# Linear attention on quarters of the TensorE array, with small matmuls kept together in the schedule

## The chip, the cores and the metric

One core of a Trainium2 chip. The metric is the device time of one execution in microseconds (us); the inputs and weights lie in the chip's main memory (HBM), the activations stay on chip. The kernel was run three times before the change: 1510.91, 1511.21 and 1512.28 us, median 1511.21. A further execution was taken with the profiler, and all rows of this document ahead of the result come from that one.

## The reference

A trunk of two layers over 512 tokens of width 1024, all in f32. Each layer: RMS norm, a mixer, a residual sum, an MLP of width 4096 with squared ReLU, then an embedding term gated by a sigmoid. Layer 1's mixer is block attention. Layer 0's mixer has two halves, 512 channels each: a gated scan ("hgrn", 4 heads of 128, computed in chunks) and the linear attention with a delta rule that the change touches ("rwkv", 8 heads of 64 channels):

```
def step(state, inp):
    r_t, w_t, k_t, v_t, kk_t, a_t = inp
    sa = einsum('bhvk,bhk->bhv', state, -kk_t)
    state = (state * w_t[:, :, None, :]
             + sa[..., None] * (kk_t * a_t)[:, :, None, :]
             + v_t[..., None] * k_t[:, :, None, :])
    return state, einsum('bhvk,bhk->bhv', state, r_t)
```

So every token's state row is decayed by w, corrected by a rank one term (kk, a) and written by (v, k), and read by r. Afterwards each head is normalised, a bonus term is added, and both halves go through one output projection.

## The kernel before

Activations lie with channels on the 128 partitions and the 512 tokens in the free dimension. All large products go through `gemm` (L248), which calls `mm3` (L243 to L246): weights and activations are split in a high and a low part of type fp32r, and each product is three matmuls of 128x128 weights by 512 streamed columns. `wnext` (L222) loads the weights on SyncE's queue (SP), and ScalarE (ACT, L236) and VectorE (DVE, L237) split them. Small jobs (the linear attention, the gated scan, statistics, transposes) use plain f32 or f16 matmuls on TensorE (PE), with their results in three rings of PSUM banks: `pj` (2 banks, gemm), `pmh` (2, gated scan) and `pmr` (4, linear attention). GpSimd (POOL) clears buffers and does some elementwise work.

The linear attention works on 4 pairs of heads (`hp`), 128 channels each, so each head has half of the partitions (`hs[h]`). The 512 tokens of a pair are taken in two halves (`g`) of 4 chunks of 64 tokens; two chunks side by side make a block `a`. There are so 8 units (hp, g). The steps of a unit:

- `pre` (L526), once for a pair: decays, the normalised key kk, beta's rows `bh`, k's rows `kh`, the receptance `rh_` and the query-like `al` (both in `ar`).
- `p1` (L588): the scores. Beta's rows of both heads are copied by ACT into `BH` (L596), whose other blocks are zero, so that one matmul for each chunk with all 128 partitions (L600) gives both heads' scores; the same for k's rows. DVE masks them into `NA` and `KA` (L605), again beside zero blocks. Four transposes for each block (L614) give `TOK` and, through ACT (L619), `BZ`, also with zero blocks. L625 and L631 multiply k's scores with v; ACT writes the second into y (L632).
- `p2` (L635): a triangular solve in f16 with five doublings (L664 to L670), one refinement in f32 (L676 to L685), and the product with the tokens (L690), copied into `MU` (L693).
- `p3` (L698): the maps of each chunk's state, on the whole array with `BZ` (L707 to L711), masked into `GB` by DVE (L714) and scaled into `HS` by ACT (L718); `inner` (L723), two groups of four matmuls with 64 columns of weights (L726, L731), added by DVE into rh_ and y (L727, L732); `states` (L735), one matmul and two DVE operations for each chunk; then the state's share of y (L754).
- `tail` (L759): normalisation and gate, and the split for the output projection.

The order of the work comes from a scheduler that builds each engine's list of instructions ahead of time, by priority among what is ready by its own cost figures. A priority follows the order of the program; `run` (L786) puts its generators 300 places ahead (`OFS`), and `weave` (L347) interleaves two generators. `ORDER` = "AFHBOC" (L33) sets the steps for each pair: A is p2 of the first half beside p3 and tail of the pair before and p1 of the second half; F and H are the projections and the gated scan; B the projections of the next pair; O the output projection of the pair before; C p2 of the second half beside `pre` of the next pair and p3 of the first half, then p1 of the next pair. Gemm passes are ranked behind and fill what PE has free. `Stats.add` (L289, L291) and `bcast_rows` (L326, L334) are helpers with groups of four small matmuls, used in both layers.

Of the kernel before, what the change touches and what calls it, by code (L numbers as in the profile page):

```python
# [12 lines left out]
F32 = mybir.dt.float32  # L13
# [6 lines left out]
OP = mybir.AluOpType  # L20
# [14 lines left out]
OFS = 300  # L35
NWARM = 9

P = 128
# [147 lines left out]
def trunk(ctx, tc, wts, xT, pT, vecs, lora, cst, lev, seg, rope, gain, out, upto="all", dbg=None, mode=None):  # L186
# [97 lines left out]
    class Stats:  # L284
# [4 lines left out]
        def add(self, sq, rhs):  # L289
            for j in range(NJ):  # L290
                T.matmul(self.ps[:, j * self.cols:(j + 1) * self.cols], sq[:, j * P:(j + 1) * P], rhs,  # L291
                         start=(self.i == 0 and j == 0), stop=(self.i == self.n - 1),
                         skip_group_check=True)
            self.i += 1
# [31 lines left out]
    def bcast_rows(rt, cols, pool, tag):  # L326
        ps = pool.tile([P, S], F32, name=tag)
        if cols > 1:
            full = nrm.tile([P, S], F32, name="bc")
            V.tensor_copy(full.rearrange("p (c w) -> p c w", w=P // cols),  # L330
                          rt[:, :, None].to_broadcast([P, NJ * cols, P // cols]))
        for j in range(NJ):
            lhs = full[:, j * P:(j + 1) * P] if cols > 1 else rt[:, j:j + 1].to_broadcast([P, P])
            T.transpose(ps[:, j * P:(j + 1) * P], lhs, ident)  # L334
        return ps
# [28 lines left out]
    def layer0_mixer(actp):  # L364
        ph = ExitStack()
        mp = ph.enter_context(tc.tile_pool(name="mp", bufs=1))
        BH = mp.tile([P, 2, 4, P], F32, name="BH")
        NAs = [mp.tile([P, 2, 2, 2, P], F32, name=f"NA{i}") for i in range(2)]
        KAs = mp.tile([P, 2, 2, 2, P], F32, name="KA")
        BZ = [mp.tile([P, 2, 2, 2, P], F32, name=f"BZ{i}") for i in range(2)]  # L370
# [3 lines left out]
        early = [BH, KAs, *NAs, *BZ, GB, SB, PP]  # L374
# [141 lines left out]
        def four(lhs, rhs):  # L516
            ps = pmr.tile([P, S], F32, name="pmr")
            for i in range(4):
                T.matmul(ps[:, i * P:i * P + P], lhs(i), rhs(i), start=True, stop=True)
            return ps.rearrange("p (i t) -> p i t", i=4)  # L520
# [5 lines left out]
        def pre(hp, r, k, v):  # L526
# [38 lines left out]
            V.tensor_mul(kk, kk, ps)  # L565
            yield
# [9 lines left out]
            V.tensor_mul(bh, bh, pi)  # L576
# [5 lines left out]
            V.tensor_mul(kh, kh, pi)  # L582
            pre_[hp] = (lw, bh, kh, ar, rh_, bo, dl, v, E("y", 2))
# [4 lines left out]
        def p1(hp, g):  # L588
            lw, bh, kh, ar, rh_, bo, dl, v, y = pre_[hp]
            gs = slice(g * 256, g * 256 + 256)  # L590
            NA, KA, TOK = NAs[g], KAs, []
            un[hp, g] = (NA, TOK)

            for n, (src, dst) in enumerate(((bh, NA), (kh, KA))):
                for h in range(2):
                    A.copy(BH[hs[h], n, :, hs[h]], src[hs[h], gs].rearrange("p (c t) -> p c t", t=64))  # L596
                ps = pmr.tile([P, S], F32, name="pmr")
                for c_ in range(4):
                    o = g * 256 + c_ * 64
                    T.matmul(ps[:, c_ * P:c_ * P + P].rearrange("p (x t) -> p x t", x=2), BH[:, n, c_, :],  # L600
                             ar[:, :, o:o + 64], start=True, stop=True)
                pv = ps.rearrange("p (a c x t) -> p a c x t", a=2, c=2, x=2)
                for h in range(2):
# [3 lines left out]
                yield  # L607
            for a in range(2):
# [4 lines left out]
                for n, src in enumerate((ar[:, 0, :], v, bh, kh)):  # L613
                    T.transpose(ps[:, n * P:n * P + P], src[:, js], ident)  # L614
# [9 lines left out]
            for i, (a, h) in enumerate(pk):  # L624
                T.matmul(ps[:, i * 64:i * 64 + 64], KA[:, a, h, 0, :], TOK[a][:, 1, hs[h]], start=True, stop=True)  # L625
            for a in range(2):
                A.copy(TOK[a][:, 2, :], ps[:, a * P:a * P + P])
            yield
            ps = pmr.tile([P, S], F32, name="pmr")
            for i, (a, h) in enumerate(pk):  # L630
                T.matmul(ps[hs[h], a * P:a * P + P], TOK[a][:, 1, hs[h]], KA[:, a, h, 1, :], start=True, stop=True)  # L631
            A.copy(y[:, gs], ps[:, :256])  # L632
            yield

        def p2(hp, g):  # L635
# [3 lines left out]
            for a in range(2):  # L639
                A.copy(n16[:, 2 * a:2 * a + 2, :], NA[:, a, :, 0, :])  # L640
# [6 lines left out]
            for l in range(1, 6):  # L647
# [12 lines left out]
                def half4(lhs, rhs):  # L660
                    ps = pmr.tile([P, S], F32, name="pmr")
                    pv = ps[:, :256].rearrange("p (i n u) -> p i n u", i=4, u=H)
                    for i in range(4):
                        T.matmul(pv[:, i], lhs[:, i, :], rhs[:, i], start=True, stop=True)  # L664
# [10 lines left out]
            for i, (a, h) in enumerate(pk):  # L675
                T.matmul(ps[:, i * P:i * P + P], NA[:, a, h, 0, :], tt[:, i, :], start=True, stop=False)  # L676
                T.matmul(ps[:, i * P:i * P + P], id16, id16, start=False, stop=True)
# [4 lines left out]
            for i in range(4):  # L682
                T.matmul(ps[:, i * P:i * P + P], er[:, i, :], XT[:, i, :], start=True, stop=False)
                T.matmul(ps[:, i * P:i * P + P], id16, XT[:, i, :], start=False, stop=True)
# [4 lines left out]
            for i, (a, h) in enumerate(pk):  # L689
                T.matmul(ps[:, i * P:i * P + P].rearrange("p (x f) -> p x f", x=2), tt[:, i, :],  # L690
                         TOK[a][:, 0::2, hs[h]], start=True, stop=True)
            MU = E("MU", 2, [P, 2, 2, P])
            A.copy(MU.rearrange("p a x (h f) -> p a h x f", h=2),  # L693
                   ps.rearrange("p (a h x f) -> p a h x f", a=2, h=2, x=2))
            un[hp, g] = (NA, TOK, MU)
            yield

        def p3(hp, g):  # L698
            lw, bh, kh, ar, rh_, bo, dl, v, y = pre_[hp]
            NA, TOK, MU = un.pop((hp, g))  # L700
# [3 lines left out]
            for a in range(2):  # L704
                bz = BZ[g][:, a]
                ps = pmr.tile([P, S], F32, name="pmr")
# [5 lines left out]
                pv = ps.rearrange("p (x c f) -> p x c f", x=2, c=2)  # L712
                for h in range(2):
                    V.tensor_tensor(GB[hs[h], 2 * a:2 * a + 2, hs[h]], pv[hs[h], 0, :, hs[h]],  # L714
                                    cc("istack")[hs[h], None, :].to_broadcast([64, 2, 64]), op=OP.add)
                    for c_ in range(2):
                        ch = 4 * g + 2 * a + c_
                        A.activation(HS[hs[h], 2 * a + c_, :], pv[hs[h], 1, c_, hs[h]], AF.Copy,  # L718
                                     scale=dl[hs[h], ch:ch + 1])
                yield  # L720


            def inner():  # L723
                ps = pmr.tile([P, S], F32, name="pmr")
                for i, (a, h) in enumerate(pk):
                    T.matmul(ps[hs[h], a * P:a * P + P], MU[:, a, 0, hs[h]], NA[:, a, h, 1, :], start=True, stop=True)  # L726
                V.tensor_add(rh_[:, gs], rh_[:, gs], ps[:, :256])  # L727
                yield
                ps = pmr.tile([P, S], F32, name="pmr")
                for i, (a, h) in enumerate(pk):  # L730
                    T.matmul(ps[hs[h], a * P:a * P + P], MU[:, a, 1, hs[h]], NA[:, a, h, 1, :], start=True, stop=True)  # L731
                V.tensor_add(y[:, gs], y[:, gs], ps[:, :256])  # L732
# [19 lines left out]
            for c_ in range(f, 4):  # L752
                ch = 4 * g + c_
                T.matmul(ps[:, c_ * 64:c_ * 64 + 64], SB[:, ch, :], rh_[:, ch * 64:ch * 64 + 64], start=True, stop=True)  # L754
# [4 lines left out]
        def tail(hp):  # L759
            lw, bh, kh, ar, rh_, bo, dl, v, y = pre_.pop(hp)  # L760
# [37 lines left out]
        def hgrn(h, q, ff, iv, gproj):  # L798
# [3 lines left out]
            for j in range(NJ):  # L802
                T.transpose(ps[:, j * P:j * P + P], iv[:, j * P:j * P + P], ident)
# [25 lines left out]
            for j in range(NJ):  # L829
                js = slice(j * P, j * P + P)  # L830
                T.matmul(ps[:, js], ks[:, js], d[:, js], start=True, stop=True)
            V.copy_predicated(at, m8[:, 13, None, :].to_broadcast([P, NJ, P]), j4(ps))
            for l in range(2, 7):
# [15 lines left out]
                for j in range(NJ):  # L849
                    js = slice(j * P, j * P + P)  # L850
# [496 lines left out]
```

## Time and profile before

| | us |
|---|---|
| median of 3 runs | 1511.21 |
| the profiled execution | 1511.89 |
| its span, first to last instruction | 1510.1 |
| PE busy | 1478.1 (98%) |
| DVE busy | 937.6 (62%) |
| ACT busy | 663.1 (44%) |
| POOL busy | 138.4 (9%) |

The span is what the profile covers, and all windows and starts are counted from its beginning. PE's busy time is made of matmul records that overlap, so work is better counted from one start to the next. An f32 matmul has two records, a transpose, an f16 or an fp32r matmul has one. PEld is PE's loading of weights, which overlaps its matmuls. The layer 0 mixer ends near 440 us.

### The profile page before, as it was taken

Reading aid. Unit: us, or ns where it says so; the run is one execution under the profiler, and the core shown is the slowest. Engines: PE = TensorE matmul, PEld = TensorE weight load, DVE = VectorE, ACT = ScalarE, POOL = GpSimd, SP = SyncE. Lnnn points to the kernel's source line nnn. Section 1 sums busy time; section 2 is a strip of 40 time slices with the busy share of each in tenths; the row PEclk is TensorE's granted clock in tenths of the full one; section 3 lists DMA queues with packets and bytes.
Section 4 is the critical chain, followed back from the end, with each engine's and each line's share of the span. In section 5 each row is a group of like instructions: output and inputs, shape, how many; then the busy total and the mean of one; then the engine's idle time right before and its main releaser. Section 6 shows DMA issues by size and latency. Waiting matters only on the chain.

```text
span 1510.1 us, 20495 instructions
## 1 busy us (share of the span) xinstructions
PE 1478.1 (98%) x7546; PEld 1191.3 (79%) x7546; DVE 937.6 (62%) x1835; ACT 663.1 (44%) x1269; POOL 138.4 (9%) x133
## 2 busy tenths in 40 slices
PE   8899999999989999999999999999999999999998
PEld 6678777777667888888888888777778888888887
DVE  6878797687785664444446648377575444445463
ACT  4675545554446433333334534455634333333342
POOL 4121220310205000000000200000220000000000
PEclk9999999999999999999999999999999999999999
DMA  5110111211123233333333432221123333333331
GB/s 179 56 36 22 55 50 39 66 29 47 39 91 106 90 98 98 98 98 98 98 95 98 124 118 84 77 63 50 56 80 95 95 101 98 98 96 93 98 98 70
DMA packets 67109, 123.88 MB, mean 82 GB/s; under 512 B 7632, under 2 KB 8016, under 8 KB 67008
## 3 DMA queue, kind: packets, MB, share of 16 engines
q1 hardware_dynamic: 65376, 118.57, 25.6%
q10 hardware_dynamic: 1152, 2.43, 0.5%
q0 software_dynamic: 480, 1.57, 0.3%
q8 instruction: 59, 0.97, 0.3%
q14 instruction: 42, 0.34, 0.1%
HBM read 120.45 MB, written 2.10 MB: 81 GB/s over the span
## 4 chain that ended last, share of the span: by engine, by line
PE 87%; DVE 7%; ACT 3%; issue 2%; DMA 1%; POOL 1%; SPq 0%; DVEq 0%; ACTq 0%; POOLq 0%
PE pj L244 20%; PE pj L246 20%; PE pj L245 20%; PE pmr L1273 1%; PE pmr L245 1%; PE pmr L1249 1%; PE pmr L246 1%; PE pmr L244 1%; PE pj L1176 1%; PE pmr L1176 1%; PE pj L1178 1%; PE pmr L1177 1%; PE pmr L1178 1%; PE pj L1177 1%; PE pmh L1176 1%
## 5 line engine op out<-in xcount | busy, mean ns | idle before, releaser
L236 ACT CAST whi<-wr 128x512 fp32r<-128x512 f32 x428 | 265.0, 621 | 549.2 <-PE pj L245 421.9
L237 DVE TENSOR_TENSOR wlo<-wr,whi 128x512 fp32r<-128x512 f32 x428 | 312.5, 733 | 197.6 <-ACT whi L236 193.6
L244 PE MATMUL pj<-act,whi 128*128 128x512 f32 (+1 forms) x856 | 338.1, 396 | 1.2 <-DVE h L935 1.0
L245 PE MATMUL pj<-act,whi 128*128 128x512 f32 (+1 forms) x856 | 336.8, 394 | 0.0
L246 PE MATMUL pj<-act,wlo 128*128 128x512 f32 (+1 forms) x856 | 335.7, 393 | 0.5 <-DVE wlo L237 0.5
L244 PE MATMUL pj<-hid,whi 128*128 128x512 f32 x512 | 199.2, 389 | 0.0
L245 PE MATMUL pj<-hid,whi 128*128 128x512 f32 x512 | 199.2, 389 | 0.0
L246 PE MATMUL pj<-hid,wlo 128*128 128x512 f32 x512 | 199.2, 389 | 0.0
L244 PEld LDWEIGHTS pj<-act,whi 128*128 128x128 f32 x856 | 161.1, 188 | 34.4 <-ACT k L491 1.4
L246 PEld LDWEIGHTS pj<-act,wlo 128*128 128x128 f32 x856 | 161.2, 188 | 32.5 <-DVE wlo L237 1.5
L245 PEld LDWEIGHTS pj<-act,whi 128*128 128x128 f32 x856 | 161.2, 188 | 31.1 <-issue 1.5
L1115 DVE TENSOR_TENSOR x<-x,pj 128x512 f32<-128x512 f32 x128 | 88.0, 688 | 80.6 <-PE pj L246 80.2
L245 PEld LDWEIGHTS pj<-hid,whi 128*128 128x128 f32 x512 | 96.1, 188 | 20.0
L244 PEld LDWEIGHTS pj<-hid,whi 128*128 128x128 f32 x512 | 96.1, 188 | 19.9
L246 PEld LDWEIGHTS pj<-hid,wlo 128*128 128x128 f32 x512 | 96.1, 188 | 19.9
L319 POOL TENSOR_TENSOR acc<-acc,xsq 128x512 f32<-128x512 f32 x35 | 48.7, 1393 | 628.8 <-ACT xsq L313 616.0
L1104 DVE SCALAR_TENSOR_TENSOR r<-pj,rb 128x512 f32<-128x512 f32 x56 | 38.7, 691 | 84.0 <-PE pj L246 84.0
L278 DVE TENSOR_TENSOR hid<-r,hid 128x512 fp32r<-128x512 f32 x64 | 44.3, 691 | 41.5 <-ACT hid L277 41.4
L1105 ACT ACTIVATE r<-r 128x512 f32<-128x512 f32 x64 | 40.5, 632 | 21.6 <-DVE r L1104 21.5
L277 ACT CAST hid<-r 128x512 fp32r<-128x512 f32 x64 | 39.8, 621 | 1.9
L280 ACT ACTIVATE act<-x,vec 128x512 fp32r<-128x512 f32 x32 | 22.9, 720 | 29.4 <-DVE x L1133 12.7
L244 PE MATMUL pj<-os,whi 128*128 128x512 f32 x64 | 28.3, 445 | 4.4 <-DVE x L946 2.8
(387 smaller groups left out, 2225.8 us busy)
## 6 DMA issues: line engine op xcount, KB each, us to landing
wr<-in_wts_dram SPq DMA_DIRECT2D x428, 256.0 KB, 2.7
x<-in_xT_dram SPq DMA_DIRECT2D x8, 256.0 KB, 6.3
sr<-in_wts_dram SPq DMA_DIRECT2D x8, 256.0 KB, 5.3
out_dram<-x SPq DMA_DIRECT2D x7, 256.0 KB, 2.0
r<-in_pT_dram ACTq DMA_DIRECT2D x4, 256.0 KB, 3.0
lw<-in_lora_dram POOLq DMA_DIRECT2D x4, 192.0 KB, 3.1
tq<-in_rope_dram ACTq DMA_DIRECT2D x1, 512.0 KB, 6.7
tk<-in_rope_dram ACTq DMA_DIRECT2D x1, 512.0 KB, 7.6
```

Of the source, the lines that this page charges most:

```text
L236: A.copy(hi, raw)
L237: V.tensor_sub(lo, raw, hi.bitcast(F32))
L244: T.matmul(ps, wh, xh, start=first, stop=False)
L245: T.matmul(ps, wh, xl, start=False, stop=False)
L246: T.matmul(ps, wl, xh, start=False, stop=last)
L277: A.copy(h, src)
L278: V.tensor_sub(l, src, h.bitcast(F32))
L319: G.tensor_add(self.t, self.t, sq)
L1104: V.scalar_tensor_tensor(r, q, 0.0, nf[0], op0=OP.max, op1=OP.mult)
L1105: A.activation(r, r, AF.Square)
L1115: V.tensor_add(x[k], x[k], ps)
L1176: T.matmul(ps[j], xh, wh, start=k == 0, stop=False)
```

## The change

Scores are computed on quarters of the array: a matmul takes one head's 64 partitions and writes 64 partitions of the output, 16 of them for a unit instead of 8, into two banks `pq`, one for each head. Which half of the output partitions it writes depends on the chunk (`c_`), and is the other one for k's rows (`c_ ^ n`). Beta's and k's rows lie in one tile `bk`, chunk by chunk, so that one transpose (still two for each block) brings both to the partitions of a chunk (`BKs`). `W` holds for each chunk the solved rows on one half of the partitions and v's rows on the other (v with its chunks swapped is `vx`), so the separate product with v (L631) falls away: `p3` and `inner` contract over both at once, with 64 columns of weights and 64 streamed columns. BH, BZ and MU go; NA and KA lose the part that is now in `RRs`. HS is scaled by one DVE operation, the first write of y in `inner` becomes an ACT copy.

`tight()` ranks instructions 40 places ahead. It is put around the new groups and, besides them, around the small groups of `Stats.add`, `bcast_rows`, `four`, `half4`, the refinement, the state's share of y, and the gated scan (`hgrn`).

The diff, cut to its core:

```diff
+TIGHT = 40
+    def tight():
+        return tc.high_priority(offset=TIGHT)
...
         def add(self, sq, rhs):
-            for j in range(NJ):
-                T.matmul(self.ps[:, j * self.cols:(j + 1) * self.cols], sq[:, j * P:(j + 1) * P], rhs,
+            with tight():
+                for j in range(NJ):
+                    T.matmul(self.ps[:, j * self.cols:(j + 1) * self.cols], sq[:, j * P:(j + 1) * P], rhs,
...
-        BH = mp.tile([P, 2, 4, P], F32, name="BH")
-        NAs = [mp.tile([P, 2, 2, 2, P], F32, name=f"NA{i}") for i in range(2)]
-        KAs = mp.tile([P, 2, 2, 2, P], F32, name="KA")
-        BZ = [mp.tile([P, 2, 2, 2, P], F32, name=f"BZ{i}") for i in range(2)]
+        NAs = [mp.tile([P, 2, 2, P], F32, name=f"NA{i}") for i in range(2)]
+        KAs = mp.tile([P, 2, 2, P], F32, name="KA")
+        RRs = [mp.tile([P, 2, 2, 2, 64], F32, name=f"RR{i}") for i in range(2)]
+        BKs = [mp.tile([P, 2, 2, P], F32, name=f"BK{i}") for i in range(2)]
+        Ws = [mp.tile([P, 2, 2, 2, P], F32, name=f"W{i}") for i in range(2)]
...
+            vx = E("vx", 1)
+            for c_ in range(2):
+                A.copy(vx.rearrange("p (j c t) -> p j c t", c=2, t=64)[:, :, 1 - c_],
+                       v.rearrange("p (j c t) -> p j c t", c=2, t=64)[:, :, c_])
...
-            for n, (src, dst) in enumerate(((bh, NA), (kh, KA))):
-                for h in range(2):
-                    A.copy(BH[hs[h], n, :, hs[h]], src[hs[h], gs].rearrange("p (c t) -> p c t", t=64))
...
-                    T.matmul(ps[:, c_ * P:c_ * P + P].rearrange("p (x t) -> p x t", x=2), BH[:, n, c_, :],
-                             ar[:, :, o:o + 64], start=True, stop=True)
...
+            pq = [pmr.tile([P, S], F32, name="pmr").rearrange("p (c a x t) -> p c a x t", c=2, a=2, x=2)
+                  for h in range(2)]
+            with tight():
+                for a in range(2):
                     for c_ in range(2):
-                        V.tensor_tensor(dst[hs[c_], :, h, :, hs[c_]], pv[hs[h], :, c_, :, :],
-                                        tri[hs[h], None, :, :].to_broadcast([64, 2, 2, 64]), op=OP.mult)
+                        o = g * 256 + a * P + c_ * 64
+                        for n in range(2):
+                            at = bk[:, 2 * g + a, 3 * c_ if n == 0 else 1 + c_, :]
+                            for h in range(2):
+                                T.matmul(pq[h][hs[c_ ^ n], c_, a], at[hs[h]], ar[hs[h], :, o:o + 64],
+                                         start=True, stop=True)
...
-                for c_ in range(2):
-                    A.copy(BZ[g][hs[c_], a, :, c_, :], pv[hs[c_], 2:4, :])
+                A.copy(BKs[g][:, a], pv[:, 2:4, :])
+                for c_ in range(2):
+                    A.copy(W_[hs[1 - c_], a, c_, 1, :], pv[hs[1 - c_], 1, :])
...
-                T.matmul(ps[hs[h], a * P:a * P + P], TOK[a][:, 1, hs[h]], KA[:, a, h, 1, :], start=True, stop=True)
-            A.copy(y[:, gs], ps[:, :256])
...
-                T.matmul(ps[:, :256], MU[:, a, 0, :], bz[:, 0].rearrange("p c f -> p (c f)"), start=True, stop=True)
-                for c_ in range(2):
-                    o = ps[:, 256 + c_ * P:256 + c_ * P + P]
-                    T.matmul(o, bz[:, 0, c_, :], MU[:, a, 1, :], start=True, stop=False)
-                    T.matmul(o, bz[:, 1, c_, :], TOK[a][:, 1, :], start=False, stop=True)
...
+            with tight():
+                for k in range(4):
+                    a, c_ = divmod(k, 2)
+                    for h in range(2):
+                        T.matmul(pv[hs[h], k, 0], W_[:, a, c_, 0, hs[h]], BKs[g][:, a, c_, hs[h]], start=True, stop=True)
+                    for h in range(2):
+                        T.matmul(pv[hs[h], k, 1], BKs[g][:, a, c_, hs[h]], W_[:, a, c_, 1, hs[h]], start=True, stop=True)
...
-                        A.activation(HS[hs[h], 2 * a + c_, :], pv[hs[h], 1, c_, hs[h]], AF.Copy,
-                                     scale=dl[hs[h], ch:ch + 1])
+            V.tensor_tensor(HS, pv[:, :, 1, :], dl[:, 4 * g:4 * g + 4, None].to_broadcast([P, 4, 64]), op=OP.mult)
...
-                    T.matmul(ps[hs[h], a * P:a * P + P], MU[:, a, 0, hs[h]], NA[:, a, h, 1, :], start=True, stop=True)
...
-                    T.matmul(ps[hs[h], a * P:a * P + P], MU[:, a, 1, hs[h]], NA[:, a, h, 1, :], start=True, stop=True)
-                V.tensor_add(y[:, gs], y[:, gs], ps[:, :256])
+                with tight():
+                    for x_ in range(2):
+                        for a in range(2):
+                            for c_ in range(2):
+                                for h in range(2):
+                                    T.matmul(pv[hs[h], x_, 2 * a + c_], W_[:, a, c_, x_, hs[h]], RR[:, a, h, c_, :],
+                                             start=True, stop=True)
+                yield
                 V.tensor_add(rh_[:, gs], rh_[:, gs], ps[:, :256])
+                A.copy(y[:, gs], ps[:, 256:])
```

## Rows read from the trace of the kernel before

**Rows 1.** The page: busy share of PE, and its granted clock in 40 slices.
```profile
PE 1478.1 (98%) x7546; PEld 1191.3 (79%) x7546; DVE 937.6 (62%) x1835; ACT 663.1 (44%) x1269; POOL 138.4 (9%) x133
...
PEclk9999999999999999999999999999999999999999
```

**Rows 2.** Windows; columns: stretch, length, busy us (instructions) of each engine, clock, DMA.
```profile
65.00:345.00 280.00, 272.95 (x1993) 216.99 (x1992) 220.02 (x527) 159.81 (x363) 54.62 (x54) 1.00 0.14 42
345.00:430.00 85.00, 79.20 (x537) 60.06 (x536) 62.05 (x156) 35.47 (x81) 10.54 (x10) 1.00 0.15 44
...
120.00:160.00 40.00, 38.85 (x340) 32.36 (x340) 32.83 (x96) 22.22 (x59) 3.76 (x4) 1.00 0.11 30
200.00:220.00 20.00, 19.37 (x160) 15.36 (x159) 18.04 (x49) 8.41 (x17) 5.60 (x7) 1.00 0.12 35
...
440.00:445.00 5.00, 4.72 (x15) 3.44 (x15) 2.67 (x6) 1.75 (x3) 0.00 (x0) 0.75 0.34 109
```

**Rows 3.** Timeline of PE: start, length, line, out<-in, weights, streamed, records [idle before <-releaser].
```profile
64.26 2.02 PE L600 MATMUL pmr<-ar,BH 128*128 128x128 f32 x16 [0.96 <-issue]
66.12 0.27 PE L614 MATMUL pmr<-cs,ar 128*128 128x128 f32 x1
...
69.05 0.43 PE L631 MATMUL pmr<-KA,TOK 128*64 128x128 f32 x2
69.41 0.49 PE L245 MATMUL pj<-act,whi 128*128 128x512 f32 x1
...
76.77 1.08 PE L625 MATMUL pmr<-TOK,KA 128*128 128x64 f32 x8
77.78 0.66 PE L631 MATMUL pmr<-KA,TOK 128*64 128x128 f32 x8
78.38 0.29 PE L664 MATMUL pmr<-PP,XT 128*128 128x64 f16 x4
...
94.12 0.59 PE L707 MATMUL pmr<-BZ,MU 128*128 128x256 f32 x2
...
95.44 0.83 PE L831 MATMUL pmh<-h 128*128 128x128 f32 x6
...
134.43 0.44 PE L631 MATMUL pmr<-KA,TOK 128*64 128x128 f32 x4
134.80 0.29 PE L664 MATMUL pmr<-PP,XT 128*128 128x64 f16 x4
...
438.14 0.72 PE L244 MATMUL pj<-os,whi 128*128 128x512 f32 x2 [1.65 <-ACT os L277]
```

**Rows 4.** Weight loads of two lines: count, shortest/median/longest ns, first and last start, form.
```profile
L726 PEld LDWEIGHTS pmr<-NA,MU x64: 132/137/138, 110.2 to 414.5; 128*64 128x64 f32 x64
...
L600 PEld LDWEIGHTS pmr<-ar,BH x128: 186/192/193, 64.2 to 345.9; 128*128 128x128 f32 x128
```

**Rows 5.** DVE groups, 35 to 430 us: count | busy us, mean ns | idle before, releaser.
```profile
L605 DVE TENSOR_TENSOR NA<-pmr,cs 64x256 f32<-64x256 f32 x32 | 13.5, 420 | 1.9 <-PE pmr L600 1.5
...
L714 DVE TENSOR_TENSOR GB<-pmr,cs 64x128 f32<-64x128 f32 x32 | 9.2, 288 | 21.5 <-PE pmr L711 18.6 <-ACT HS L718 2.4
...
L732 DVE TENSOR_TENSOR y<-y,pmr 128x256 f32<-128x256 f32 x8 | 3.4, 419 | 3.0 <-PE pmr L731 2.9
```

**Rows 6.** ACT groups of the same stretch.
```profile
L718 ACT ACTIVATE HS<-pmr,dl 64x64 f32<-64x64 f32 x64 | 16.4, 303 | 18.0 <-DVE GB L714 17.1
...
L619 ACT COPY BZ<-pmr 64x256 f32<-64x256 f32 x32 | 11.7, 366 | 0.2
...
L596 ACT COPY BH<-bh 64x256 f32<-64x256 f32 x16 | 6.4, 402 | 8.4 <-PE pmr L600 4.3 <-DVE bh L576 4.0
...
L617 ACT COPY TOK<-pmr 128x256 f32<-128x256 f32 x16 | 5.9, 372 | 2.2 <-PE pmr L614 1.9
...
L693 ACT COPY MU<-pmr 128x512 f32<-128x512 f32 x8 | 4.7, 584 | 6.8 <-PE pmr L690 6.8
...
L627 ACT COPY TOK<-pmr 128x128 f32<-128x128 f32 x16 | 3.4, 267 | 1.2 <-PE pmr L625 1.1
```

More of the change, by code (lines that the diff above doesn't have):

```diff
@@ L517, in four @@
             ps = pmr.tile([P, S], F32, name="pmr")
-            for i in range(4):
-                T.matmul(ps[:, i * P:i * P + P], lhs(i), rhs(i), start=True, stop=True)
+            with tight():
+                for i in range(4):
+                    T.matmul(ps[:, i * P:i * P + P], lhs(i), rhs(i), start=True, stop=True)
             return ps.rearrange("p (i t) -> p i t", i=4)
@@ L638, in p2 @@
             n16 = E("n16", 1, [P, 4, P], F16)
-            for a in range(2):
-                A.copy(n16[:, 2 * a:2 * a + 2, :], NA[:, a, :, 0, :])
+            A.copy(n16, NA.rearrange("p a h t -> p (a h) t"))
             X = E("X", 1, [P, 4, P], F16)
@@ L662, in half4 @@
                     pv = ps[:, :256].rearrange("p (i n u) -> p i n u", i=4, u=H)
-                    for i in range(4):
-                        T.matmul(pv[:, i], lhs[:, i, :], rhs[:, i], start=True, stop=True)
+                    with tight():
+                        for i in range(4):
+                            T.matmul(pv[:, i], lhs[:, i, :], rhs[:, i], start=True, stop=True)
                     return pv
@@ L688, in p2 @@
             ps = pmr.tile([P, S], F32, name="pmr")
[L689 to L695, printed above, removed]
+            with tight():
+                for i, (a, h) in enumerate(pk):
+                    T.matmul(ps[:, i * P:i * P + P].rearrange("p (x f) -> p x f", x=2), tt[:, i, :],
+                             TOK[a][:, 0::2, hs[h]], start=True, stop=True)
@@ L751, in p3 @@
             f = 1 if g == 0 else 0
-            for c_ in range(f, 4):
-                ch = 4 * g + c_
-                T.matmul(ps[:, c_ * 64:c_ * 64 + 64], SB[:, ch, :], rh_[:, ch * 64:ch * 64 + 64], start=True, stop=True)
+            with tight():
+                for c_ in range(f, 4):
+                    ch = 4 * g + c_
+                    T.matmul(ps[:, c_ * 64:c_ * 64 + 64], SB[:, ch, :], rh_[:, ch * 64:ch * 64 + 64], start=True, stop=True)
             yg = y[:, g * 256 + f * 64:g * 256 + 256]
@@ L828, in hgrn @@
             ps = pmh.tile([P, S], F32, name="pmh")
-            for j in range(NJ):
-                js = slice(j * P, j * P + P)
-                T.matmul(ps[:, js], ks[:, js], d[:, js], start=True, stop=True)
+            with tight():
+                for j in range(NJ):
+                    js = slice(j * P, j * P + P)
+                    T.matmul(ps[:, js], ks[:, js], d[:, js], start=True, stop=True)
             V.copy_predicated(at, m8[:, 13, None, :].to_broadcast([P, NJ, P]), j4(ps))
@@ L848, in hgrn @@
                 ps = pmh.tile([P, S], F32, name="pmh")
-                for j in range(NJ):
-                    js = slice(j * P, j * P + P)
-                    T.matmul(ps[:, j * 64:j * 64 + 64], ks[:, js], qs[:, j * 64:j * 64 + 64], start=True, stop=True)
+                with tight():
+                    for j in range(NJ):
+                        js = slice(j * P, j * P + P)
+                        T.matmul(ps[:, j * 64:j * 64 + 64], ks[:, js], qs[:, j * 64:j * 64 + 64], start=True, stop=True)
                 def hi(t):
@@ L871, in hgrn @@
             ps = pmh.tile([P, S], F32, name="pmh")
-            for j in range(3):
-                T.matmul(ps[:, j * P:j * P + P], kt[:, j * P:j * P + P], vt[:, j, :], start=True, stop=True)
+            with tight():
+                for j in range(3):
+                    T.matmul(ps[:, j * P:j * P + P], kt[:, j * P:j * P + P], vt[:, j, :], start=True, stop=True)
             st_ = Hh()
```

130 lines of the change are left out of this document (73 added, 57 removed).

## The prediction

> **What bounds the kernel now.** I read the page's busy shares and slices first, then windows of the stretch that the diff touches, then the timeline of TensorE inside it, then the groups of VectorE and ScalarE there. The page shows TensorE (PE) busy in 98% of the span and at full clock almost throughout [rows 1]. The linear attention and the gated scan beside it lie between 35 and about 440 us. In the windows from 65 to 430 us PE is busy for 352.2 of 365 us, VectorE (DVE) for 282.1, ScalarE (ACT) for 195.3 [rows 2]. So PE bounds this stretch. But DVE is close in places: 32.8 of 40 us where the chains of two head pairs meet (120 to 160 us), 18.0 of 20 us in the window from 200 to 220 us [rows 2]. A microsecond taken from PE is therefore a microsecond of time only while DVE, and the chain PE to DVE to ACT and back, still keep up.
>
> How PE's time is counted: start to start, not by the busy durations, which hold a pipeline's tail. An f32 matmul is two records. Sixteen records of the old scores (128 columns streamed, whole array) take from 64.26 to 66.12 us, 0.116 us each [rows 3]. Eight records with only 64 columns streamed (L625) take from 76.77 to 77.78 us, 0.126 each including the way into the next group [rows 3]: halving the streamed columns alone gains nothing when 128 columns of weights are loaded. The weight loads differ: median 192 ns for 128 columns, 137 ns for 64 [rows 4], so 64 columns of weights cost 55 ns and 128 cost 110, which is what the small matmuls are paced by.
>
> The rows that matter most are those of matmuls that fill half of the array's columns (L631). One such matmul alone (x2) takes from 69.05 to 69.41 us, 0.36; two, one in each half (x4), from 134.43 to 134.80, 0.37; four (x8), from 77.78 to 78.38, 0.60 [rows 3]. The second is free: the halves run side by side. Two further pairs of records cost 0.23 us, so a slot of two records of 128 streamed columns takes about 0.11, and a group of four slots has 0.60 - 0.42 = 0.18 us of edges at 0.105 a slot. The entry from whole-array work costs some 0.09 more: L625's eight records at 0.112 would have ended 0.9 us after their start, and the gap is 1.01 [rows 3]. A group that uses part of the array thus costs 0.27 us plus its slots.
>
> **The change, part by part.** There are eight units, one for each of 4 head pairs and 2 halves of the sequence.
>
> Scores (p1). Removed: 8 matmuls, 16 records, 1.86 us [rows 3]. Added: 16 matmuls of 64 rows by 64 columns, 32 records; four neighbours lie on four different quarters of the array. No row shows quarters split by rows. Bounds: if all four run side by side, 8 slots, 0.84 + 0.27 = 1.11 us; if only column halves do, 16 slots, 1.68 + 0.27 = 1.95; if none do, 32 slots, 3.36 + 0.27 = 3.63. I take 1.11, because the nearest row (L631) shows the other way of splitting fully overlapped, and each half of the rows has an output bank of its own here.
>
> The Trainium skill (TensorEngine Tiling (Array Packing), Key Properties) says that a change of tiling mode drains the engine and that tiles load and multiply independently; the entry of 0.09 us and the free second matmul agree. The Trainium skill (TensorE: Matmul & The Clock Gate, Part 3: Packing small matmuls) also says that matmuls start and end in strict program order. By that rule a matmul's second record, on the same quarter as its first, would hold back the next quarter, and every matmul would need a slot.
>
> Worked out from rows, one slot for each matmul would make two matmuls cost 0.36 + 0.105 = 0.47 us; the trace has 0.37 [rows 3]. So I do not use it for the sum; its price, 1.95 instead of 1.11 a unit, is in the rivals.
>
> The four matmuls of k's rows against v (L631) go away: 0.60 + 0.09 = 0.69 us. Their result now comes out of the matmuls of inner(), because v's rows sit beside the solved rows in W.
>
> State maps (p3). Removed: from 94.12 to 95.44 us, 1.32 us, twice: 2.64 [rows 3]. Added: 16 matmuls with 64 columns of weights and 64 streamed, pairs on the two column halves: 16 slots. A slot is bounded below by the load of 64 columns, 0.055 [rows 4], above by the old slot of 0.105; nearest is the load, since L625 shows loads pacing short streams. 16 x 0.055 + 0.27 = 1.15 (above: 1.95).
>
> inner(). Removed: L726 and L731, each a group like L631 at 0.69, 1.38 us. Added: one group like the new p3: 1.15 (above: 1.95).
>
> Sum of a unit: 1.86 + 0.69 + 2.64 + 1.38 = 6.57 before; 1.11 + 1.15 + 1.15 = 3.41 after; 3.16 saved, 25.3 us in eight units. The transposes keep their count (8 a unit, now with beta's and k's rows of a chunk side by side), and so do the solver's matmuls.
>
> Grouping. The scheduler cuts L631 and L731 apart in some units; a matmul left alone, as the one at 69.05 us, pays its own edges [rows 3]. I count 9 such extra pieces in the trace, 0.27 us each, 2.4 us. For matmuls on the whole array the order changes little, because L600's neighbours follow at 0.1 us; the grouping of statistics, transposes and scan matmuls I cost at nothing (between -2 and +2 us, the size of one such wait in either direction), covered by gemm passes that stand ready beside them. That cover is missing around 435 us, where all of x must be finished.
>
> DVE, each unit: masks of the scores, 8 x 420 ns, become 8 x 288 (64x128, as L714) and 2 x 419 (128x256, as L732): 3.36 to 3.14. GB: 4 x 288 to 2 x 419; one more 419 for HS, taken over from ACT; L732's sum goes: 1.57 to 1.26 [rows 5]. About 0.5 us less, 4 us in all. ACT: gone are 4 copies into BH (0.402), 4 into BZ (0.366), 8 scalings into HS (16.4 us over 64, 0.256) and one MU copy (0.584), 5.7 us; new are 2 copies to BK (0.372), 4 of v into W (0.267), 2 into W (0.584) and one of vx for each unit (0.402), 3.4 us [rows 6]. About 18 us less in all. ACT did not bound the stretch, so this shortens chains only. y moves from a DVE sum to an ACT copy of the same size. No DMA is added or moved except that POOL clears less before it issues the load of the constants; they are first used at the first broadcast near 36 us, behind the gemm passes, so I cost this at nothing. p1 now holds two pmr banks at once instead of one after the other; of four, two are left for the solver, which uses at most two at a time. If that cover fails, the solver waits for about 3 us of DVE masks in a unit, which is the second rival.
>
> What is late next: 27.7 us less PE work in the units. From 120 to 160 us lie two p1 and one p3 with its inner(): 2 x (1.86 + 0.69 - 1.11) + 2.64 + 1.38 - 2.30 = 4.6 us saved, which leaves 35.4 us with some 32 of DVE work, 90% busy. The window from 200 to 220 us works at that share already and PE is still busy in 19.4 of 20 us [rows 2], so it is no floor, but waits grow. I take three quarters of 27.7, 21 us; this quarter is an estimate from that share.
>
> The profiled execution took 1511.9 us with a span of 1510.1; the median of the runs is 1511.2, 0.7 below it. 1511.2 - 21 = **1490.5 us**.
>
> **The rivals.**
> First, quarters overlap by columns only, or one slot for each matmul: scores cost 1.95, 6.7 us of the gain go: (27.7 - 6.7) x 3/4 = 16, 1495.5. With no overlap of quarters at all, 3.63, it is 1505.5. For it: no row with half of the rows. Against: L631's free second matmul.
> Second, DVE and the chain keep the length: PE's relief turns into waits wherever gemm passes are scarce (120 to 160, 220 to 260, 320 to 360, 400 to 430 us), and counts only beside gemm passes, for about a third of the work: 9 us, 1502. For it: the DVE shares [rows 2]. Against: PE's busy share in the same windows.
> Third, slower: neither rows nor columns overlap in the new groups, because with streams of 64 columns each record is paced by its own load. Place: the three new groups. Price: 3.63 + 2 x (32 x 0.055 + 0.27) = 7.69 a unit against 6.57, 9 us more, 1520. It decides once a unit's groups exceed 6.57 us. Against: the two loads of a pair at 134.43 us would then have to show up as time, and they do not.
> Fourth, the change does little: the grouping delays gemm passes behind producers, and its waits cancel the gain; 1511.
> A fall of the clock is a risk and not a case of its own: the granted clock was 0.75 of full from 440 to 445 us, after PE had waited 1.65 us for the inputs of the last projections at 438.14 [rows 2, 3], and full in the other windows of rows 2.
>
> **How the numbers follow.** Forecast 0.55, column overlap only 0.13, no quarter overlap 0.05, DVE and the chain 0.14, no change 0.05, slower 0.08. What this kernel's measurement can tell from no change is about 0.2%, 3 us. Faster by more than that: 0.55 + 0.13 + 0.05 + 0.14, less 0.03 for their tails: 0.84; same 0.07; slower 0.09. The range reaches down to all of 27.7 us with 5 us of shorter chains (1478) and up past the rivals at 1502 and 1505.5, to 1508. The forecast's own range is 1482 to 1498.
>
> **What would show it.** Right: a score group of 32 records in about 1.1 us; p3's and inner()'s groups of 32 in about 1.15 each; no L631-like pieces alone; BH, BZ and HS gone from ACT; PE still above 95% busy from 65 to 420 us and the span shorter by the end of layer 0, with layer 1 as before. Wrong: score groups near 2 or 3.6 us (rivals one and three); idle PE in front of solver matmuls that wait for DVE (rival two); a gap before the first MLP passes that is longer, or a lower granted clock.

## The result: 0.6% slower, with the profile after

The changed kernel takes 1520.07 us (median of 4 runs, 1518.01 to 1520.74) against 1511.06 for the kernel before beside it: ratio 1.0056, interval 1.0039 to 1.0074. That is 9 us slower, where 20.7 less were forecast, and outside the range. The page of the profiled execution (1520.74 us) has these lines:

```profile
span 1519.0 us, 21017 instructions
PE 1471.4 (97%) x7834; PEld 1187.1 (78%) x7834; DVE 927.8 (61%) x1835; ACT 643.8 (42%) x1197; POOL 139.2 (9%) x132
PEclk9999999999989999999999999999999999999999
```

The work shrank: ACT by 19.3 us, DVE by 9.8, PE's busy time by 6.7, with 288 more records [rows 1]. But PE is idle for 47.6 us of the span (1519.0 - 1471.4), against 32.0 before. Two windows of [rows 2], and four short ones (same columns):

```profile
65.00:345.00 280.00, 266.05 (x2161) 209.51 (x2160) 211.78 (x521) 141.19 (x302) 55.81 (x53) 0.98 0.14 42
345.00:430.00 85.00, 79.68 (x627) 63.17 (x627) 61.78 (x150) 35.72 (x74) 11.28 (x10) 0.94 0.17 51
...
110.00:115.00 5.00, 3.28 (x30) 2.53 (x30) 4.71 (x16) 1.75 (x4) 1.85 (x3) 0.93 0.04 14
115.00:120.00 5.00, 5.00 (x60) 4.38 (x56) 2.50 (x7) 1.18 (x4) 1.10 (x1) 0.73 0.00 0
...
415.00:420.00 5.00, 3.07 (x20) 2.81 (x20) 5.00 (x11) 1.29 (x3) 2.65 (x2) 0.81 0.00 0
420.00:425.00 5.00, 4.43 (x20) 3.96 (x20) 2.50 (x7) 1.10 (x2) 0.00 (x0) 0.50 0.42 134
```

From 65 to 430 us PE is busy for 345.7 of 365 us (94.7%, 96.5% before), and its granted clock, full before [rows 2], is 0.98 and 0.94. The dips stand behind waits of PE: at 113.47 us it had waited 1.72 us for the solver's X, at 417.41 us 1.52 us for the gated scan, and the windows behind these have 0.73 and 0.50; half is the lower of the clock's two levels. The two waits in PE's timeline:

```profile
113.47 0.22 PE L692 MATMUL pmr<-X,n 128*128 128x64 f16 x2 [1.72 <-DVE X L697]
...
417.41 1.33 PE L887 MATMUL pmh<-qs,KS 128*128 128x64 f32 x8 [1.52 <-DVE KS L882]
```

The timeline of PE in the middle of a unit (columns as in [rows 3]; the scores are L622, the solver's f16 groups `half4` L692, y's state share L787) shows why PE does no better with less to do. First a score group that was left whole, then one that was not:

```profile
130.53 1.10 PE L622 MATMUL pmr<-ar,bk 64*64 64x128 f32 x32
131.56 0.33 PE L640 MATMUL pmr<-cs,ar 128*128 128x128 f32 x1
...
145.68 0.43 PE L622 MATMUL pmr<-ar,bk 64*64 64x128 f32 x2
146.04 0.20 PE L692 MATMUL pmr<-X,n 128*128 128x64 f16 x1
146.08 0.41 PE L787 MATMUL pmr<-ar,SB 128*128 128x64 f32 x2
146.42 0.65 PE L622 MATMUL pmr<-ar,bk 64*64 64x128 f32 x8
147.00 0.23 PE L692 MATMUL pmr<-PP,XT 128*128 128x64 f16 x2
147.07 0.41 PE L787 MATMUL pmr<-ar,SB 128*128 128x64 f32 x2
147.32 0.19 PE L692 MATMUL pmr<-PP,XT 128*128 128x64 f16 x1
147.44 0.43 PE L622 MATMUL pmr<-ar,bk 64*64 64x128 f32 x2
147.80 0.20 PE L692 MATMUL pmr<-PP,XT 128*128 128x64 f16 x1
...
150.45 0.43 PE L622 MATMUL pmr<-ar,bk 64*64 64x128 f32 x2
150.81 0.20 PE L692 MATMUL pmr<-X,n 128*128 128x64 f16 x1
```

The whole group takes 1.03 us, start to start. The second unit's 32 records stand in eight pieces between 145.68 and 150.81 us; two records alone take 0.36 us (145.68 to 146.04) where eight take 0.58 (146.42 to 147.00). In PE's instruction list the 24 new groups (three kinds, eight units) stand in 78 pieces; the 24 old half-column groups L631, L726 and L731 stood in 34.

An edge appears without a change of tiling mode too (of the part of the array that a matmul uses). In the kernel before, a gemm pass between single solver records, all on the whole array, takes 0.32 us start to start, 0.09 more than among other gemm passes (0.23, from 164.15 to 164.38 us):

```profile
165.35 0.48 PE L245 MATMUL pj<-act,whi 128*128 128x512 f32 x1
165.67 0.20 PE L664 MATMUL pmr<-PP,XT 128*128 128x64 f16 x1
```

At the first MLP norm a second loss stands. PE's timeline there in the changed kernel (L297 are the statistics):

```profile
467.61 1.05 PE L297 MATMUL pmh<-ones,acc 128*128 128x1 f32 x8 [3.66 <-POOL acc L325]
...
473.18 0.39 PE L249 MATMUL pmh<-act,whi 128*128 128x512 f32 x1
```

And the same place in the kernel before (L291):

```profile
464.66 1.05 PE L291 MATMUL pmh<-ones,acc 128*128 128x1 f32 x8 [0.77 <-POOL acc L319]
465.57 0.49 PE L244 MATMUL pmh<-act,whi 128*128 128x512 f32 x1
```

The statistics, ranked ahead, stand in PE's list after 947 gemm passes (matmuls of `mm3`) instead of 960. PE waits 3.66 us at them for POOL, with 13 gemm passes queued behind that ran ahead of them before. From the 937th pass to the 961st, the first behind the norm, it took 7.3 us before and takes 11.9 after; the passes behind the long wait run at a lower clock too, 0.73 from 470 to 475 us.

### The profile page after: what moved, and what is told of

Read it like the earlier page. It is cut to its first block, busy times and chain, and to the rows that moved or that the text cites. A ratio compares the mean times of both kernels' runs of the same rounds, so it can differ in the third digit from the quotient of the medians.

```text
span 1519.0 us, 21017 instructions
## 1 busy us (share of the span) xinstructions
PE 1471.4 (97%) x7834; PEld 1187.1 (78%) x7834; DVE 927.8 (61%) x1835; ACT 643.8 (42%) x1197; POOL 139.2 (9%) x132
## 4 chain that ended last, share of the span: by engine, by line
PE 67%; DVE 2%; POOL 1%; ACT 1%; issue 0%; POOLq 0%; ACTq 0%; DVEq 0%
PE pj L249 17%; PE pj L250 17%; PE pj L251 17%; PE pmr L1313 1%; PE pmr L1289 1%; PE pj L1216 1%; PE pj L1218 1%; PE pj L1217 1%; PE pmh L1216 1%; PE pmh L1218 1%; PE pmh L1217 1%; PE pmr L1218 1%; PE pmr L1216 1%; PE pmr L1217 1%; PE pmr L249 1%; PE pmr L251 1%
## 5 line engine op out<-in xcount | busy, mean ns | idle before, releaser
L250 PEld LDWEIGHTS pj<-hid,whi 128*128 128x128 f32 x512 | 96.1, 188 | 20.1
L249 PEld LDWEIGHTS pj<-hid,whi 128*128 128x128 f32 x512 | 96.1, 188 | 20.1
L286 DVE SCALAR_TENSOR_TENSOR act<-x,vec,act 128x512 fp32r<-128x512 f32 x32 | 27.8, 876 | 12.5 <-ACT act L285 12.5
```

## The experiments

The theory: the quarters are worth what was forecast while their groups stay whole; ranking every small job by the same 40 places interleaves the groups of different generators, and each cut costs edges, by the theory changes of tiling mode. Rivals: the early statistics; the earlier load of constants; slow quarters. In these kernels `whole()` stands for `tight()` around the scores, p3's maps and inner(), so that the two can be ranked apart; later lines have numbers higher by 4. Ratios are to the kernel before, timed on the same chip. The runs are spread over several chips; differences in us are between medians, and by the ratios they come out up to 1.6 us otherwise.

**No ranking at all.** All of the change's arithmetic, program order.
```diff
 def tight():
-    return tc.high_priority(offset=TIGHT)
+    return ExitStack()
+def whole():
+    return ExitStack()
```


> The changed kernel without any ranking of small jobs. The list has 60 pieces of the new groups, the statistics stand where they stood before the change. Theory A: 18 pieces fewer than in the changed kernel, 5 us, and the norms' 6 us: about 1509 us, between the changed kernel and the one with only the groups ranked. Theory C: the same time as with only the groups ranked, within 2 us.

Measured: 1499.15 us, 0.9915 (0.9899 to 0.9930), 60 pieces. The arithmetic gains 12 us without any ranking; the ranking as it stands costs 21. Both expectations missed: the ranking was dearer than the pieces and the norms had made it, and the kernel with the groups alone ranked (next) is 8.2 us faster still.

**Only the new groups ranked**; called the second kernel from here on.
```diff
 def tight():
-    return tc.high_priority(offset=TIGHT)
+    return ExitStack()
+def whole():
+    return tc.high_priority(offset=40)
```


> The changed kernel, with the rank of 40 places only around its three new groups of matmuls (scores, state maps, inner), and none around the other small jobs. Each of the new groups then stands whole in TensorE's list, 25 pieces instead of 78 for 24 groups. Theory A: 53 pieces fewer at some 0.27 us each are 14 us, and the norms' 6 us: about 1500 us, faster than both kernels. Theory C: DVE and the chain set the length of the stretch, the pieces lie in time that is waited anyway, and only the norms' part is won: about 1513 us, with more idle TensorE or more time at the low clock before 440 us.

Measured: 1490.98 us, 0.9864 (0.9848 to 0.9881), 25 pieces. This is 9 us below the expectation and the forecast's time, and the fastest kernel together with two below. Its page:

```profile
span 1488.3 us, 20991 instructions
PE 1452.5 (98%) x7834; PEld 1172.1 (79%) x7834; DVE 932.0 (63%) x1835; ACT 641.4 (43%) x1197; POOL 138.7 (9%) x132
```

The groups of PE between 35 and 430 us (count | busy us, mean ns | idle before) hold the same instructions in the changed kernel and in this one. First the changed kernel: scores, two of the solver's three groups, inner(), p3's two.

```profile
L622 PE MATMUL pmr<-ar,bk 64*64 64x128 f32 x256 | 16.3, 281 | 1.8 <-DVE bk L595 1.8
L692 PE MATMUL pmr<-X,n 128*128 128x64 f16 x160 | 15.8, 195 | 1.9 <-DVE X L697 1.7
L692 PE MATMUL pmr<-XT,PP 128*128 128x64 f16 x160 | 15.5, 194 | 0.2 <-ACT W L651 0.2
...
L760 PE MATMUL pmr<-RR,W 128*64 128x64 f32 x256 | 14.8, 239 | 0.0
...
L741 PE MATMUL pmr<-BK,W 128*64 128x64 f32 x128 | 11.6, 233 | 0.0
...
L743 PE MATMUL pmr<-W,BK 128*64 128x64 f32 x128 | 9.3, 228 | 0.0
```

And the second kernel, the solver's first:

```profile
L696 PE MATMUL pmr<-X,n 128*128 128x64 f16 x160 | 15.2, 196 | 3.5 <-DVE X L701 3.5
L696 PE MATMUL pmr<-XT,PP 128*128 128x64 f16 x160 | 13.6, 196 | 1.6 <-ACT W L655 1.6
...
L626 PE MATMUL pmr<-ar,bk 64*64 64x128 f32 x256 | 9.3, 276 | 0.3 <-DVE bk L599 0.3
L764 PE MATMUL pmr<-RR,W 128*64 128x64 f32 x256 | 9.2, 225 | 0.0
L745 PE MATMUL pmr<-BK,W 128*64 128x64 f32 x128 | 9.1, 240 | 0.0
...
L747 PE MATMUL pmr<-W,BK 128*64 128x64 f32 x128 | 8.7, 234 | 0.0
```

The mean of one record is much alike (281 and 276 ns for the scores). But the same 256 score records keep PE busy for 16.3 us in pieces and 9.3 us whole, because records that overlap count once. The four lines of new groups have 15.7 us less in sum here, 0.30 for each of the 53 pieces that are gone; the solver's three, no longer interleaved with them, have 4.6 less (its third takes 15.2 and 13.1). Of the 30.7 us between the two spans, 18.9 are PE's busy time and 11.8 its idle time, which is 35.8 us here.

**Statistics back at their old rank**, all else as in the change.
```diff
     def add(self, sq, rhs):
-            with tight():
+            with ExitStack():
```


> The changed kernel, with the statistics of the norms (Stats.add) at their old rank; all else is as changed. Theory A (the ranking costs the time): in the changed kernel the statistics stand in TensorE's list ahead of gemm passes that are ready (after 947 passes instead of 960 at the first MLP norm), and TensorE stands 3.66 us before them; the slip between the two kernels grows by 3.6 us there and by 2.3 us more in layer 1. All this should go: about 1514 us. Theory C (the chain of the linear attention bounds, whatever is ranked): the wait only moves to the next consumer of the norm, about 1519 us.

Measured: 1506.46 us, 0.9965 (0.9953 to 0.9977), 75 pieces: 13.6 us below the changed kernel, and below both expectations.

**Statistics ranked beside the new groups alone**, in the second kernel.
```diff
     def add(self, sq, rhs):
-            with tight():
+            with whole():
```


> The kernel with only the three new groups ranked, and the statistics of the norms ranked 40 places ahead as well. The new groups stay whole (25 pieces), the statistics stand early again (after 61, 948, 2708 and 3456 gemm passes). Theory A with the price from putting the statistics back in the changed kernel: 13.6 us more than with the groups alone, 1504.6 us. Rival: what was won there came in part from other pieces falling elsewhere, and the statistics cost only what their waits show (2.4 us at the first norm, 3.6 at the first MLP norm, 2.3 in layer 1): 1499 us.

Measured: 1492.42 us, 0.9877 (0.9861 to 0.9894), 1.4 us above that kernel, inside its interval and below both expectations. The wait for POOL is there all the same (waits of PE: total us, times, longest):

```profile
PE pmh L301 <- POOL acc L329: 4.4, 2, 3.7
```

**Statistics ranked in the kernel before**, nothing else.
```diff
     def add(self, sq, rhs):
-            for j in range(NJ):
-                T.matmul(self.ps[:, j * self.cols:(j + 1) * self.cols], ...
+            with tight():
+                for j in range(NJ):
+                    T.matmul(self.ps[:, j * self.cols:(j + 1) * self.cols], ...
```


> The kernel of before with nothing changed but the rank of the statistics. Theory A: the early statistics cost their waits whatever the linear attention looks like, 8 to 14 us, 1519 to 1525 us. Theory C: in the old kernel gemm passes or the chain hide them, 1511 us within 2.

Measured: 1510.92 us, 1.0003 (0.9990 to 1.0015): nothing. So early statistics cost next to nothing alone, and my price for them fell.

**The solver ranked beside the new groups**, in the second kernel.
```diff
-    with tight():
+    with whole():
         for i in range(4):
             T.matmul(pv[:, i], lhs[:, i, :], rhs[:, i], start=True, stop=True)
```


> The kernel with only the three new groups ranked, and the solver's groups of four (half4) ranked alike. The list then has 62 pieces of the new groups instead of 25, the statistics stay late. Theory A: 37 pieces at 0.27 us, 10 us more than with the groups alone, 1501 us. Rival: the pieces fill time in which TensorE would wait for the solver's chain, and cost nothing or gain, 1491 us or less.

Measured: 1503.16 us, 0.9955 (0.9938 to 0.9972), 62 pieces. One more ranked helper costs 12.2 us: for 37 pieces, 0.33 us each.

**All ranked by 40, but the new groups by 200.**
```diff
+def whole():
+    return tc.high_priority(offset=200)
```


> The changed kernel with its three new groups ranked 200 places ahead instead of 40, all other small jobs at 40 as changed. The only aim is to have the new groups whole (25 pieces instead of 78) while everything else keeps its rank, the early statistics too. Theory A: 53 pieces at 0.3 us are 16 us: about 1504 us, and the 13 us that are left to the kernel with only the groups ranked (1491) are the price of ranking the other jobs. If the pieces cost nothing: 1520 us.

Measured: 1501.46 us, 0.9939 (0.9922 to 0.9956), 25 pieces. With everything else ranked as in the change, keeping 24 groups whole is worth 18.6 us, 0.35 for each of 53 pieces. Its page (an execution of 1497.67 us, the fastest of its four):

```profile
span 1495.8 us, 20997 instructions
PE 1449.0 (97%) x7834; PEld 1170.8 (78%) x7834; DVE 927.4 (62%) x1835; ACT 643.2 (43%) x1197; POOL 141.0 (9%) x132
```

PE's busy time is 22.4 us below the changed kernel's, its idle time (46.8 us) nearly the same. Against the second kernel its busy time is 3.5 us less and its idle time 11.0 us more.

**The same, statistics at their old rank.**
```diff
     def add(self, sq, rhs):
-            with tight():
+            with ExitStack():
```


> The same with the statistics at their old rank. Putting them back won 13.6 us in the changed kernel, ranking them cost 1.4 us beside whole groups. If they cost that much only together with the other ranked jobs, this is about 1491 us when the run before it is 1504. If the 13.6 us came from how the pieces of the new groups fell (and from the clock that fell with them), this is within 3 us of the run before it.

Measured: 1491.16 us, 0.9864 (0.9849 to 0.9878): another 10.3 us, down to the second kernel's time. In this company the statistics do cost. PE is idle for 43.7 us of that kernel's span (1490.4 us) and busy for 1446.7, so at the second kernel's time it has more idle and less busy time than that one: idle time by itself doesn't price the ranking.

**The kernel before with all its own small jobs ranked by 40** (statistics, broadcasts, scores, solver, maps, inner(), scan; no other edit), each in this manner:
```diff
-    for i in range(4):
-        T.matmul(pv[:, i], lhs[:, i, :], rhs[:, i], start=True, stop=True)
+    with tight():
+        for i in range(4):
+            T.matmul(pv[:, i], lhs[:, i, :], rhs[:, i], start=True, stop=True)
...
```


> The kernel of before with all its small groups ranked 40 places ahead, as the change does, and nothing else of the change. Its groups on column halves (L631, L726, L731 before) stand in 64 pieces instead of 34 in the list. Theory A: 30 pieces at 0.3 us, 9 us more, about 1520 us: ranking everything alike costs the old code too. Rival: it is harmless there (1511 us) and hurts only the new groups.

Measured: 1538.09 us, 1.0174 (1.0159 to 1.0190). L631, L726 and L731 stand in 64 pieces instead of 34. Its page:

```profile
span 1534.0 us, 20499 instructions
PE 1489.1 (97%) x7546; PEld 1202.0 (78%) x7546; DVE 935.9 (61%) x1835; ACT 665.8 (43%) x1269; POOL 138.5 (9%) x133
```

PE's busy time is 11.0 us more than before, its idle time 12.9 (44.9 against 32.0). The ranking alone costs the old code 26 us, not the expected 9; between the changed kernel and the second one, where it is much the same ranking, lie 29.

**POOL's clears before the load of the constants put back** into the changed kernel.
```diff
+        G.memset(SB, 0.0)
+        G.memset(GB[:, 0:3, :], 0.0)
...
+        G.memset(SB[:, 0:8, :], 0.0)
```


> The changed kernel with GpSimd kept clearing for as long as before the change (extra clears of buffers that are cleared anyway, 1536 elements a partition ahead of the load of the constants, 1024 behind it), so that the loads of constants start as late as before. Theory B (the earlier loads of constants take bandwidth from x at the start): the first gemm pass into pj, at 35.45 us in the changed kernel and at 33.16 before the change, comes back by about 2 us, and the time falls to about 1518 us. Rival: that delay is the statistics ranked ahead at the first norm; then nothing changes here, 1520 us, and the delay goes with the statistics put back.

Measured: 1520.45 us, 1.0058 (1.0043 to 1.0073). The earlier load plays no part, as costed.

**Scores issued head by head** in the second kernel, so that neighbours in the list have only two quarters, not four.
```diff
-    for a in range(2):
-        for c_ in range(2):
-            for n in range(2):
-                for h in range(2):
+    for h in range(2):
+        for a in range(2):
+            for c_ in range(2):
+                for n in range(2):
```


> The kernel with only the three new groups ranked, and the scores issued for all of one head (one half of the array's rows) before the other head; the two column halves still alternate. If quarters run side by side only where neighbours in the list lie on different quarters, a group of 32 records takes 16 slots, 1.95 us instead of 1.03, 0.9 us for each of eight units: 1498 us. If each quarter takes its records from far ahead in the list, a group still takes about 1.1 us, 1491 us.

Measured: 1490.28 us, 0.9867 (0.9852 to 0.9881). A score group takes 1.53 us start to start, between the two expectations, which in eight units is 4 us more of PE that the time does not show. PE's timeline in this kernel:

```profile
69.41 1.60 PE L626 MATMUL pmr<-ar,bk 64*64 64x128 f32 x32
70.94 0.34 PE L534 MATMUL pmr<-id,XT 128*128 128x128 f16 x3
```

And in the second kernel, where the group takes 1.04 us:

```profile
67.43 1.10 PE L626 MATMUL pmr<-ar,bk 64*64 64x128 f32 x32
68.47 0.34 PE L534 MATMUL pmr<-id,XT 128*128 128x128 f16 x3
```

## Why the prediction was wrong

**Scores, maps, inner(): right.** 1.03 us for a score group (1.11 forecast). p3's 32 records take 1.08 us in the second kernel (1.15 forecast), and so do inner()'s (108.11 to 109.19 us). Its timeline at p3:

```profile
93.03 0.34 PE L745 MATMUL pmr<-BK,W 128*64 128x64 f32 x4
...
93.89 0.29 PE L747 MATMUL pmr<-W,BK 128*64 128x64 f32 x4
94.11 0.26 PE L696 MATMUL pmr<-X,n 128*128 128x64 f16 x3
```

The rivals with slow quarters (the first and the third) are out: the third's time, 1520, came, but not by its mechanism.

**DVE and ACT: right.** L627 takes 288 ns (288 forecast), L746 420 (419), and L748, HS, 424 (419) [rows 5]; ACT's BK 376 (372), v into W 260 (267), W 580 (584) [rows 6]. In the second kernel DVE's busy time is 5.6 us less than before (4 forecast), ACT's 21.7 (18). The second rival is out too, since the second kernel gains the forecast 20 us with the same work on DVE. The groups of DVE in the changed kernel (columns as in [rows 5]):

```profile
L627 DVE TENSOR_TENSOR NA<-pmr,cs 64x128 f32<-64x128 f32 x32 | 9.2, 288 | 4.9 <-PE pmr L622 4.4
...
L746 DVE TENSOR_TENSOR GB<-pmr,cs 64x256 f32<-64x256 f32 x16 | 6.7, 420 | 10.8 <-PE pmr L743 10.7
...
L748 DVE TENSOR_TENSOR HS<-pmr,dl 128x256 f32<-128x256 f32 x8 | 3.4, 424 | 0.2
```

**Three quarters of 27.7 us: right, once the groups are whole.** 20.1 us came (1511.06 - 1490.98). The forecast took the missing quarter, about 7 us, as waits. In the profiled runs PE's busy time is 25.6 us less than before, 27.7 forecast, with 3.5 us more of clock withheld (below), and its idle time is 3.8 us more. So the total fits better than its parts. POOL's earlier load, costed at nothing, measured nothing.

**Grouping: wrong, and the whole of the miss.** The step took it that `tight()` makes each new group whole, gained 2.4 us by it (for 9 extra pieces; the old list has 10), and costed the ranking of all other small jobs between -2 and +2 us. It measured 29 us: 1520.07 for the change, 1490.98 with the ranking around the new groups alone. I had read a rank as "ahead of the rest"; but the solver, the scan, the transposes and the statistics got the same 40 places. The new groups kept no lead over them, and stand in more pieces (78) than without any ranking (60). Pricing it needed only the row that I had: the lone half-column matmul that takes 0.36 us [rows 3]. By the step's own edge of 0.27 us, 53 extra pieces would have cost 14.3 us; by the runs a piece costs 0.23 (no ranking against groups only, 8.2 us for 35 pieces) to 0.35 us. The other small jobs, which the step had at nothing, cost the rest when they are ranked too: 10.5 us (1501.46 against 1490.98) with all new groups whole, of which 10.3 go when the statistics alone are put back. The unknown that I bounded by "one such wait" had an upper end of tens of microseconds, and slower a far larger chance than 0.09.

The fourth rival was the right kind (grouping cancels the gain) at the wrong size, with a chance of 0.05: it ended at no change, and its price was waits behind producers. Those came too, PE's idle time being 15.6 us more than before, but between the changed kernel and the second one they are the smaller part (11.8 of 30.7 us); the largest single wait that the trace shows is the 3.66 us at the MLP norm.

**The clock.** I named its fall a risk and gave it no case; of the signs named as wrong, it came and so did the longer gap before the first MLP passes (3.66 us of waiting, 0.77 before), and of the signs of being right, PE above 95% and no pieces alone failed. Summed over the whole stretches of 5 us in the span, the part of full clock not granted, times 5 us, makes 5.1 us before, 17.0 in the changed kernel and 8.6 in the kernel with only the new groups ranked. These are single profiled executions, and 3.4 of the 17.0 lie before 35 us, where x arrived late in that execution; such a start also came with the scores in turn and not in the second kernel, with the same code there, and not in the changed kernel with POOL's clears put back, so it is taken as scatter. It is part of the 29 us, not to be added to the pieces: what a kernel with fewer pieces gains holds both.

**What stays open.** The statistics cost 0 or 1.4 us alone and 10 to 14 beside other ranked jobs, while the profiles show some 5 us at the norm (11.9 - 7.3). The rest was not found. Nor do cuts explain all of the old code's 26 us: 30 extra pieces at 0.35 are 10.5, close to the 11.0 us of added busy time, and the 12.9 us of idle time are beside them. Which part of a piece's price is the change of tiling mode and which is some other edge was not measured. That equal ranks are what interleaves the generators is read from the lists and fits all piece counts; the scheduler's choices themselves were not followed one by one.

## What to carry to other kernels

A priority works only against what does not have it: rank the few groups that must stay together, by themselves or above other ranked work (with the statistics among it, that cost 10.3 us here), and count in the instruction list whether they did. Work that uses part of the array costs by the piece, so price a change of schedule by pieces and edges before taking it as free. When a change joins new arithmetic with a new order, forecast the two apart, and bound the order by the worst cut, not by one wait.

## What the hardware showed beyond that

Quarters split by rows run side by side in full: by the prediction's edge and slot, 1.03 us are (1.03 - 0.27) / 0.105 = 7.2 slots for 32 records on four quarters. In the second kernel's trace the first records of all four quarters start within 0.02 us, and later fours follow at 0.11 us. Issued head by head, with only two quarters among near neighbours, the group is (1.53 - 0.27) / 0.105 = 12 slots, between the 8 of four quarters at once and the 16 of two. In the trace of that kernel the second head's first pair of records starts 0.51 us behind the first head's, with three of the first head's eight pairs still to start. So, if the list keeps the order of the edit, PE takes some matmuls from further back beside the ones in front, but the second head's eight do not all run beside the first's. That the 0.5 us a unit did not show in the time fits gemm passes that had room elsewhere; no run tested it. The Trainium skill (TensorE: Matmul & The Clock Gate, Part 3: Packing small matmuls) says that matmuls start and end in strict program order; one slot for each f32 matmul, 16 of them, would follow from that as I read it, and both groups are faster. The Trainium skill (TensorEngine Tiling (Array Packing), Key Properties) says that a change of tiling mode drains the engine; the 0.36 us of a lone pair of records agree, but no run here shows the drain apart from other edges.
